# Operands of the recurrences turned tokens-first by VectorE and a DRAM round trip instead of by TensorE, with decays and late turnings put elsewhere

## The chip, the cores and the metric

The kernel runs on one core of a Trainium2 chip. The metric is the time of one execution on the device, in microseconds; lower is better. One profiled execution gives the trace that the profile is made of.

## The reference, cut to what matters

One step of a two-layer hybrid trunk with D = 2048: 256 prompt tokens from a zero state and 8 sequences of 8 sample tokens from given states, 320 tokens in all. Layer 0 projects the normalised input once and runs two recurrences on parts of it; layer 1 is a gated linear recurrence (RG-LRU). All is float32.

```python
proj = einsum('btd,de->bte', rmsnorm(x), w_in)          # Q, K, V of DeltaNet; gates; Q, K, V of GLA ...
q, k, v = silu(causal_conv(qkv))                        # 8 heads x 128
q = q * rsqrt(sum(q*q) + 1e-6) * 128**-0.5
k = k * rsqrt(sum(k*k) + 1e-6)
beta = sigmoid(b_raw);  g = -exp(a_log) * softplus(a_raw + dt_bias)
# gated delta rule, S (128 x 128) for each head:
S_t = exp(g_t) S_{t-1} (I - beta_t k_t k_t^T) + beta_t k_t v_t^T;   o_t = S_t^T q_t
# GLA, S (128 x 256) for each of 4 heads, gk = log_sigmoid(lr @ w_lr + b_lr) / 16:
S_t = diag(exp(gk_t)) S_{t-1} + k_t v_t^T;                          o_t = S_t^T q_t
x = x + concat(rmsnorm(o_a)*silu(z_a), rmsnorm(o_b)*silu(z_b)) @ w_out
x = x + (rg_lru(conv(x w_x)) * silu(x w_g)) @ w_lru_out
```

The delta rule is computed in chunks: with decays, k k^T and q k^T of a chunk give a triangular matrix, whose inverse is applied to the values. Final states and convolution histories are outputs too.

## The kernel before, in words

Activations lie with channels on the 128 partitions and tokens along the free dimension. The dense work is 30 groups of 512 output columns. A group has eight 512 KB weight chunks, loaded on SyncE's DMA queue (`wst`, three buffers, `load_chunk`, L214); each half of a chunk is split into a high and a low part, `wh` by ScalarE (L248) and `wl` by VectorE (L249), with six buffers each, and every product is three matmuls of 128x128 by 128x320 on L382 (xh wh, xl wh, xh wl). That is 5760 matmuls, called the main products here, and they run from beginning to end of the program. The groups come in the order Q0, K0, V0, V1, K1, Q1 (DeltaNet's, first and second half of the heads), QB, KB, VB, VB (GLA's), four gate groups, four of w_out, eight of the RG-LRU's input and four of its output.

Everything else is woven between them. The recurrences are Python generators in queues (`hi`, `lo`, `lo2`, `tails`). After every third main product `slot()` advances each queue by one step, and the table `WAITS` says for how many slots a named step waits. So the order on TensorE is written out by this table; a tile scheduler adds the semaphores, and each engine then runs its list in order. PSUM has four buffers for the groups (`acc`) and four that all the woven work shares in turn (the helpers `bank` and `bank4`): a matmul into such a buffer waits until the result four uses before has been read.

The woven work that the change touches:

- `delta_half(0)` and `delta_half(1)`: four heads each, in two chunks of 128 tokens (a "quad" is four heads of one chunk). `quad_a` turns K, Q and V tokens-first by TensorE transposes with an identity (`kt` L720, `qt` L729, `vt` L771), sums squares of K and Q on ScalarE, makes the decays between tokens (`ug` L746 on VectorE, `df` and `gr` L755 on TensorE, `dtm` and `eg` on ScalarE), then `kk` (L777) and `kq` (L789), times the decays into `bt` and `mt`. `nb`, minus beta over the norm of k, is turned (`nbt` L799) and stored. `invert32` loads the diagonal blocks from DRAM (`bd_scratch`), multiplies them by `nb` (L827) and inverts them on GpSimd; `quad_front` builds the whole inverse XT; `quad_b` and `quad_end` apply it (`y` L966) and make outputs and state.
- `delta_sample` does the same for the 8 sample sequences, with the states loaded into `st` on SyncE's queue (L1032), and the chain bt, inversion on VectorE, XT, `y` (L1074), `pq` (L1081), `ot` (L1105).
- `gla_decays` makes GLA's cumulated decays (`lrp` L1338 on TensorE, `gk`). `gla_head` turns V of GLA by TensorE (`gvt` L1443) and uses it in `gpo` (L1450) and `gsn` (L1454).

## Time and profile before

| | |
|---|---|
| runs (three) | 975.67, 975.74, 976.48 us; median 975.74 |
| profiled execution: time, span of its instructions | 975.99 us, 973.8 us |
| mean granted TensorE clock | 0.998 |
| TensorE busy | 963.4 us, 99% of the span |
| VectorE, ScalarE, GpSimd busy | 693.9, 532.8, 193.3 us |
| main products, mean duration as listed | 5568 of 128x320 on L382, 310 to 313 ns |

A matmul's listed duration is from its start to its result; several are in flight at once, so what one costs TensorE is the distance to the next start. An engine's idle time is put down to whatever released the instruction after it. The line numbers are those of the kernel before, unless a text says otherwise.

### The profile page before, as it was taken

How to read it: one execution, taken by the hardware profiler on the slowest of the kernel's cores; microseconds unless marked ns; L12 is line 12 of the kernel's file. 1: busy time of each engine (PE TensorE's matmuls, PEld its weight loads, DVE VectorE, ACT ScalarE, POOL GpSimd, SP SyncE). 2: the span in 40 equal slices, each digit the busy share in tenths (PEclk: the TensorE clock that was granted, in tenths of full speed). 3: DMA queues.
4: the chain of work that ended last, by engine and by line, in shares of the span. 5: the costliest groups of instructions: out<-in, count | busy, mean ns of one | idle time of the engine just before them, and what ended most of it. 6: DMA issues, size and time to landing. Idle time of an engine off the chain costs nothing.

```text
span 973.8 us, 18776 instructions
## 1 busy us (share of the span) xinstructions
PE 963.4 (99%) x6921; PEld 947.0 (97%) x6921; DVE 693.9 (71%) x1470; ACT 532.8 (55%) x1089; POOL 193.3 (20%) x336
## 2 busy tenths in 40 slices
PE   9999999999999999999999999999999999999996
PEld 9999999999999999999989999999999999999996
DVE  7598887666545556788668789667969668876763
ACT  7767865447333454876423345348685885333452
POOL 4010128403381011120105124100010000042200
PEclk9999999999999999999999999999999999999999
DMA  9854444533545366444587877654435435677742
GB/s 323 296 172 130 136 129 149 169 108 122 151 152 153 98 229 222 126 130 130 193 277 231 258 239 252 202 154 154 154 127 180 132 129 169 190 228 252 265 170 109
DMA packets 68123, 175.03 MB, mean 180 GB/s; under 512 B 17116, under 2 KB 26096, under 8 KB 67520
## 3 DMA queue, kind: packets, MB, share of 16 engines
q1 hardware_dynamic: 62904, 163.69, 52.8%
q0 software_dynamic: 2720, 8.66, 2.5%
q10 hardware_dynamic: 2408, 1.49, 0.5%
q8 instruction: 54, 0.88, 0.4%
q14 instruction: 37, 0.30, 0.1%
HBM read 159.14 MB, written 14.68 MB: 178 GB/s over the span
## 4 chain that ended last, share of the span: by engine, by line
PE 97%; DVE 1%; DMA 0%; issue 0%; ACT 0%; SPq 0%; POOL 0%; DVEq 0%; ACTq 0%; POOLq 0%
PE acc L382 83%; PE acc L268 3%; PE fbt L311 1%; PE gpo L1500 0%; DMA ob<-in_x_cols_dram 0%; PE lg L1689 0%; PE lg L1687 0%; PE lg L1688 0%; PE kq L789 0%; PE kk L777 0%; PE gsn L1263 0%; PE po L975 0%; PE pq L1063 0%; PE sn L1249 0%; PE y L966 0%
## 5 line engine op out<-in xcount | busy, mean ns | idle before, releaser
L382 PE MATMUL acc<-xh,wh 128*128 128x320 f32 x1856 | 580.1, 313 | 0.3 <-ACT wh L235 0.3
L382 PE MATMUL acc<-xl,wh 128*128 128x320 f32 x1856 | 574.3, 310 | 0.0
L382 PE MATMUL acc<-xh,wl 128*128 128x320 f32 x1856 | 573.4, 310 | 0.3 <-DVE wl L249 0.3
L248 ACT ACTIVATE wh<-wst 128x512 fp32r<-128x512 f32 x479 | 278.9, 624 | 299.1 <-PE acc L382 251.7
L249 DVE TENSOR_TENSOR wl<-wst,wh 128x512 fp32r<-128x512 f32 x479 | 331.6, 722 | 150.8 <-ACT wh L248 148.5
L382 PEld LDWEIGHTS acc<-xh,wh 128*128 128x128 f32 x1856 | 348.8, 188 | 3.4 <-issue 1.3
L382 PEld LDWEIGHTS acc<-xl,wh 128*128 128x128 f32 x1856 | 348.7, 188 | 1.1
L382 PEld LDWEIGHTS acc<-xh,wl 128*128 128x128 f32 x1856 | 348.2, 188 | 1.1 <-DVE wl L249 0.5
L590 DVE SCALAR_TENSOR_TENSOR yc<-slab,pa,yc 128x344 f32<-128x344 f32 x72 | 40.5, 575 | 3.0 <-ACT yc L102 2.7
L834 POOL TENSOR_TENSOR xi<-xi,tmp 128x60 f32<-128x60 f32 (+24 forms) x62 | 26.1, 421 | 4.9
L832 POOL TENSOR_TENSOR tmp<-ab,xi 128x60 f32<-128x60 f32 (+24 forms) x62 | 24.7, 398 | 4.8
L1716 POOL MEMSET aa<- 128x32 f32 x4 | 0.6, 162 | 117.7 <-ACT rr L1703 66.7
L1144 POOL TENSOR_TENSOR uvkh<-uvk,uvkh 32x256 fp32r<-32x256 f32 (+1 forms) x8 | 10.7, 1342 | 51.5 <-DVE uvkh L1140 50.6
L1149 POOL TENSOR_TENSOR uvm<-uvh,rm 96x512 fp32r<-96x512 f32 x16 | 19.5, 1241 | 2.8 <-PE sn L1249 2.5
L1253 DVE SCALAR_TENSOR_TENSOR ust<-ust,es,sn 128x128 f32<-128x128 f32 x64 | 18.2, 337 | 2.5 <-PE sn L1249 2.2
L889 POOL TENSOR_TENSOR so<-so,mhalf 128x4 f32<-128x4 f32 x4 | 4.4, 1104 | 74.0 <-DVE so L888 74.0
L268 PE MATMUL acc<-xl,wh 128*128 128x320 f32 (+1 forms) x64 | 18.7, 292 | 0.0
L268 PE MATMUL acc<-xh,wl 128*128 128x320 f32 (+1 forms) x64 | 18.7, 292 | 0.0
L594 ACT ACTIVATE qkv<-yc 128x256 f32<-128x256 f32 x24 | 10.0, 415 | 15.9 <-DVE yc L590 15.8
L268 PE MATMUL acc<-xh,wh 128*128 128x320 f32 (+1 forms) x64 | 18.6, 291 | 0.0
L1267 DVE SCALAR_TENSOR_TENSOR ugt<-ugt,ebs,gsn 128x256 f32<-128x256 f32 x32 | 14.1, 474 | 5.6 <-PE gsn L1263 5.5
L1647 DVE SCALAR_TENSOR_TENSOR yc<-slab,pb,yc 128x344 f32<-128x344 f32 x32 | 17.5, 569 | 0.6 <-ACT yc L1645 0.5
(465 smaller groups left out, 1053.1 us busy)
## 6 DMA issues: line engine op xcount, KB each, us to landing
wst<-in_w_dense_dram SPq DMA_DIRECT2D x237, 512.0 KB, 3.7
st<-in_state_delta_dram SPq DMA_DIRECT2D x8, 512.0 KB, 7.0
st<-in_state_gla_dram SPq DMA_DIRECT2D x4, 1024.0 KB, 6.9
ust<-in_state_delta_dram SPq DMA_DIRECT2D x8, 512.0 KB
out_s_delta_dram<-ust POOLq DMA_DIRECT2D x8, 512.0 KB, 4.7
ugt<-in_state_gla_dram SPq DMA_DIRECT2D x8, 512.0 KB, 5.5
out_s_gla_dram<-ugt POOLq DMA_DIRECT2D x8, 512.0 KB, 4.3
xtok<-in_x_rows_dram SPq DMA_DIRECT2D x6, 512.0 KB, 6.3
```

The costliest lines, as they stand in the source:

```text
L248: act.activation(h, wst[i][:, a, :], AF.Copy)
L249: env["last_split"] = dve.tensor_sub(l, wst[i][:, a, :], h.bitcast(F32))
L268: mm = pe.matmul(accs[f][:, cols], w[:, fs], x[:, cols], start=(k == 0 and j == 0), stop=(k == KT - 1 and j == 2), skip_group_check=True)
L382: mm = pe.matmul(o, (h, h, l)[j][:, fs], (xh, xl, xh)[j][k], start=(k == 0 and j == 0), stop=(k == KT - 1 and j == 2))
L590: dve.scalar_tensor_tensor(y[:, :n], xp[:, j:j + n], pa[:, ft, j:j + 1], y[:, :n], op0=OP.mult, op1=OP.add)
L832: behind(pool.tensor_mul(tv, ab[:, j, j + 1:, None].to_broadcast([P, m, w]), xi[:, j:j + 1, :w].to_broadcast([P, m, w])))
L834: behind(pool.tensor_add(xi[:, j + 1:, :w], xi[:, j + 1:, :w], tv))
L1144: pool.tensor_sub(o, t[rows, :, cols], o.bitcast(F32))
L1149: pool.tensor_mul(m, src.bitcast(F32)[:, None, :].to_broadcast([R, 4, P]), rm4[:R, :, None].to_broadcast([R, 4, P]))
L1253: dve.scalar_tensor_tensor(s_, s_, es[:, col:col + 1], ps[:, b, :], op0=OP.mult, op1=OP.add)
L1267: dve.scalar_tensor_tensor(s_, s_, ebs[:, h, 4 * hb + b + i:4 * hb + b + i + 1], ps[:, i * 256:(i + 1) * 256], op0=OP.mult, op1=OP.add)
L1647: dve.scalar_tensor_tensor(y[:, :n], xp[:, j:j + n], pb[:, ft, 2 + j:3 + j], y[:, :n], op0=OP.mult, op1=OP.add)
```

## The change

Eighty-one TensorE transposes are removed: `kt`, `qt`, `vt` (20 each), `nbt` (5) and `gvt` of V (16). In their place `turn` transposes 32x32 blocks on VectorE with a strided source (44 instructions), into a staging tile; SyncE's queue stores it to a DRAM scratch (`tp_scratch` for prompt tokens, `ts_scratch` for samples), and `load_turned` loads it back with its rows in tokens-first order, in runs of 512 bytes. The loaded tiles hold [token, block of 32, head, 32], so `y`, `gpo` and `gsn` read them in runs of 32 elements.

Beside this: the squares of K and Q are summed from the loaded tiles; the factor `nb` goes into `dtm` (four scalings on VectorE per quad), so that `nbt`, its store and load, and the multiplication by `bn` before the inversions go; `quad_front`'s scaling becomes a copy, half of it on ScalarE; the second chunk's `ug` is made by GpSimd; `gla_decays` starts 70 slots after its flag instead of 11; V of the first half and Q of the second half are turned and loaded after the quads (`rest`); the blocks for the inversion are stored and loaded in fewer, larger transfers; and the samples' states are loaded on ScalarE's queue.

```diff
...
-    "small_work.1": 0, "small_work.2": 2, "small_work.3": 10, "quad_a.1": 2, "quad_a.2": 8, "quad_a.3": 0,
+    "small_work.1": 0, "small_work.2": 2, "small_work.3": 10, "delta_sample.9": 3, "turn.4": 40, "turn.5": 0, "delta_sample.3": 3, "quad_a.1": 8, "quad_a.2": 2, "quad_a.3": 0,
...
+    "turn.1": 3, "turn.2": 6, "turn.3": 10, "quad_a.8": 10, "gla_decays.3": 5, "gla_decays.4": 1, "gla_decays.5": 3, "gla_decays.6": 3, "gla_decays.7": 6, "gla.1": 0,
-    "tables.2": 14, "small_work.4": 3, "small_work.5": 9, "gla_decays.8": 11, "quad_b.9": 1,
+    "tables.2": 14, "small_work.4": 3, "small_work.5": 9, "gla_decays.8": 70, "quad_b.9": 1,
...
-    nb_d = nc.dram_tensor("nb_scratch", (20, P), F32, kind="Internal").ap()
+    tp_d = nc.dram_tensor("tp_scratch", (8, 2, P, 4 * P), F32, kind="Internal").ap()
+    ts_d = nc.dram_tensor("ts_scratch", (3, 1, P, 4 * P), F32, kind="Internal").ap()
...
+    def turn(src, d, flag, to, gate, first):
+        yield from wait(first)
+        while gate not in env["done"]:
+            yield
+        n = src.shape[2] // P
+        to = to.rearrange("p f t -> p (f t)")[:, :4 * P * n].rearrange("p (c x) -> p c x", c=n)
+        for f in range(4):
+            behind(dve.transpose(to.rearrange("p c (b u j) -> p u c b j", u=4, j=32)[:, f],
+                                 src[:, f, :].rearrange("p (c i b) -> p c b i", c=n, b=4)))
+            yield from wait("turn.1")
+        yield from wait("turn.2")
+        behind(sp.dma_start(d.rearrange("c p x -> p c x"), to))
+        yield from wait("turn.3")
+        env["done"].add(flag)
+    def load_turned(out, d, c=0):
+        sp.dma_start(out.rearrange("p a u j -> p a (u j)"), d[c].rearrange("(a i) (b x) -> (i b) a x", a=4, b=4))
+    def turn_conv(part, half, to, gate):
+        first = "turn.4" if (part, half) in ((2, 0), (0, 1)) else "turn.5"
+        src = env["QKV"[part], half]
+        turns.append(turn(src, tp_d[2 * part + half], ("t", part, half), to, gate, first))
+    def turn_sample(part):
+        src = env["SMP" + "QKV"[part]].rearrange("p u q e x -> p u (q e x)")
+        turns.append(turn(src, ts_d[part], ("t", part, "s"), ob[3], "gd", "turn.5"))
...
+            def turned():
+                if part or half:
+                    turn_conv(part, half, ob[1], "x0")
+                if part == 1 and half == 0:
+                    turn_conv(0, 0, ob[0], "x0")
+                if half:
+                    turn_sample(part)
+            hi.append(later(turned))
...
+        turned = lambda part: (tp_d[2 * part + half], c) if q.n == 32 else (ts_d[part], 0)
         ss = t("ss", [P, 8])
-        ps = bank4("kt")
-        for u in range(U):
-            pe.transpose(ps[:, u, :], q.k(u), ident)
-        q.ktm = t("ktm")
-        act.activation(q.ktm, ps, AF.Copy)
-        for u in range(U):
-            j = t("junk", [P, P], 1)
...
-        ps = bank4("qt")
-        for u in range(U):
-            pe.transpose(ps[:, u, :], q.q(u), ident)
...
+        rows = lambda nm, tag=None: t(nm, [P, 4, 4, 32], tag=tag)
+        kin = rows("kin", "mt")
+        if q.n < 32:
+            q.bt = t("bt")
+        load_turned(kin, *turned(1))
+        late = {0: 2, 1: 0}.get(half)
+        if late != 0:
+            qin = q.bt.rearrange("p u (a j) -> p u a j", j=32)
+            load_turned(qin, *turned(0))
+        if late != 2:
+            q.rv = rows("rv")
+            load_turned(q.rv, *turned(2))
         if q.n == 32:
...
-            ug = ws.tile([P, 2, 4, P], F32R, name="ug", tag="ab", bufs=1)
+            ug = ws.tile([P, 2, 4, P], F32R, name="ug", tag=("ab", "XT")[c], bufs=1)
...
-            dve.tensor_mul(ug[i], q.um[:, None, :].to_broadcast([P, 4, P]),
+            (pool if c else dve).tensor_mul(ug[i], q.um[:, None, :].to_broadcast([P, 4, P]),
...
+        q.ktm = t("ktm")
+        act.activation(q.ktm.rearrange("p u (a j) -> p a u j", j=32), kin, AF.Copy)
+        for u in range(U):
+            j = t("junk", [P, P], 1)
+            act.activation(j, q.ktm[:, u, :], AF.Square, accum_out=ss[:, u:u + 1])
...
+        def v_scale():
+            dve.tensor_mul(q.rv, q.rv, q.bk[:, None, :, None].to_broadcast([P, 4, 4, 32]))
+        dve.tensor_scalar(sk, sk, EPS, None, op0=OP.add)
+        dve.reciprocal(q.nb, sk)
+        dve.scalar_tensor_tensor(q.nb, q.nb, -1.0, beta[:, q.gc:q.gc + 4], op0=OP.mult, op1=OP.mult)
+        for u in range(U):
+            dve.scalar_tensor_tensor(dt[:, u, :], dt[:, u, :], q.nb[:, u:u + 1], q.um, op0=OP.mult, op1=OP.mult)
+        pool.tensor_tensor(q.bk, sk, mhalf[:, :4], OP.pow)
+        pool.tensor_mul(q.bk, q.bk, sk)
+        pool.tensor_scalar(q.bk, q.bk, -1.0, None, op0=OP.mult)
...
-        ps = bank4("vt")
-        for u in range(U):
-            pe.transpose(ps[:, u, :], q.v(u), ident)
-        q.rv = t("rv")
-        scaled4(q.rv, ps, q.bk, NA0)
-        yield from wait("quad_a.4")
...
-        ps = bank("nbt")
-        pe.transpose(ps[:4, :P], q.nb, ident)
-        nbt = t("nbt", [4, P], 1)
-        act.activation(nbt, ps[:4, :P], AF.Copy)
-        pool.dma_start(nb_d[q.id:q.id + 4, :], nbt)
...
+        def rest():
+            while ("t", late, half) not in env["done"]:
+                yield
+            x = rows("rv") if late else rows("qin", "pt")
+            load_turned(x, *turned(late))
+            yield from wait("quad_a.8")
+            if late:
+                q.rv = x
+                v_scale()
+            else:
+                q_sums(x)
+            env["done"].add(("rows", q.id))
+        if late is not None:
+            lo2.append(rest())
...
-        pool.tensor_mul(ab, ab, bn[:, None, :].to_broadcast([P, n, n]))
...
-        def scale(ps, rows, w):
-            for c, q in enumerate(qs):
-                dve.tensor_mul(pt[c][rows, :, :w], ps[rows, 4 * c:4 * c + 4, :w],
-                               q.nb[rows, :, None].to_broadcast([rows.stop - rows.start, 4, w]))
+        def keep(ps, rows, w):
+            dve.tensor_copy(pt[0][rows, :, :w], ps[rows, 0:4, :w])
+            act.activation(pt[1][rows, :, :w], ps[rows, 4:8, :w], AF.Copy)
...
-            pe.matmul(ps[:, u, :], q.xt[:, u, :], q.rv[:, u, :], start=True, stop=True)
+            pe.matmul(ps[:, u, :], q.xt[:, u, :], q.rv[:, :, u, :], start=True, stop=True)
...
+            yield from wait("delta_half.2")
+            for b, bs in enumerate(blocks):
+                sp.dma_start(bd_d[us, b].rearrange("u j i -> j u i"), bt[bs, :, bs])
...
-                    sp.dma_start(st[:, e], state_delta[2 * u + e])
+                    act.dma_start(st[:, e], state_delta[2 * u + e])
+            yield from quad_a(q, ws, 1)
+            inverse = invert(ws, 4, 8)
+            next(inverse)
+            yield from wait("delta_sample.9")
             load(0)
             load(1)
-            yield from quad_a(q, ws, 1)
-            yield from invert(ws, 4, 8)
+            yield from inverse
             load_inv(q, ws)
...
+                if pr == 0:
+                    yield from wait("delta_sample.3")
+                    load(2)
+                    load(3)
...
-            pt = bank4("gvt")
-            for hf in range(2):
-                vt = 2 * h + hf
-                pe.transpose(pt[:, hf, :], env["VB", vt // 4][:, vt % 4, cs], ident)
-            pe.transpose(pt[:, 2, :], kd[128][:, cs], ident)
-            vk = t("gvk", [P, 3, P])
-            act.activation(vk, pt[:, :3], AF.Copy)
+            pt = bank("gvt")
+            pe.transpose(pt[:, :P], kd[128][:, cs], ident)
+            vk = t("gvk", [P, P])
+            act.activation(vk, pt[:, :P], AF.Copy)
             yield from wait("gla.3")
             po = bank("gpo")
-            vtm = vk[:, 0:2, :].rearrange("p a b -> p (a b)")
-            pe.matmul(po[:, :256], at, vtm, start=True, stop=not c)
+            split = lambda x: x[:, :256].rearrange("p (f a j) -> p f a j", f=2, j=32)
+            vtm = vt[c][:, :, 2 * (h % 2):2 * (h % 2) + 2, :].rearrange("p a f j -> p f a j")
+            pe.matmul(split(po), at, vtm, start=True, stop=not c)
             if c:
...
-                yield from weave(gla_head(h, ws), gla_head(h + 1, ws))
+                while ("t", "VB", h // 2) not in env["done"]:
+                    yield
+                vt = [ws.tile([P, 4, 4, 32], F32, name="gvv", tag="gvv", bufs=4) for _ in range(2)]
+                for c in range(2):
+                    load_turned(vt[c], tp_d[6 + h // 2], c)
+                yield from weave(gla_head(h, ws, vt), gla_head(h + 1, ws, vt))
...
```

Three places of the order. First TensorE at the first two quads (half 0), with the main products between the rows left out. Before:

```order
L755 MATMUL df<-ug,sl_r 128x512 x2
L771 MATMUL vt<-ident,qkv 128x128 x4
L777 MATMUL kk<-qkv 128x128 x4
L789 MATMUL kq<-qkv 128x128 x4
L799 MATMUL nbt<-ident,nb 4x128
L382 MATMUL acc<-xh_118,wh 128x320
L382 MATMUL acc<-xl_134,wh 128x320
L382 MATMUL acc<-xh_118,wl 128x320
L755 MATMUL df<-ug,sl_r 128x512 x2
L755 MATMUL gr<-ug,ones_r 128x512 x2
```

With the change:

```order
L794 MATMUL df<-ug,sl_r 128x512 x2
L794 MATMUL gr<-ug,ones_r 128x512 x2
L384 MATMUL acc<-xh_117,wh 128x320
L384 MATMUL acc<-xl_133,wh 128x320
L384 MATMUL acc<-xh_117,wl 128x320
L1409 MATMUL lrp<-lr_231 128x320
...
L831 MATMUL kk<-qkv 128x128 x4
L838 MATMUL kq<-qkv 128x128 x4
L831 MATMUL kk<-qkv 128x128 x4
L838 MATMUL kq<-qkv 128x128 x4
```

The first df stands three main products ahead of this piece, and six more main products stand where rows are left out. kk and kq of both quads are now one after another, after both df; a row of GLA's decays (lrp) has come between, and the transposes are gone.

Second, TensorE at the samples' first two head pairs: the end of pq, its output's transpose ot, and the second pair's pq. Before, with 36 main products between the first two rows:

```order
L1081 MATMUL pq<-y_4877,mt 128x256 x2
...
L1105 MATMUL ot<-ident,on 128x128 x2
L382 MATMUL acc<-xh_111,wh 128x320
L382 MATMUL acc<-xl_127,wh 128x320
L382 MATMUL acc<-xh_111,wl 128x320
L1063 MATMUL pq<-st,qm 32x128 x32
```

With the change, 22 main products:

```order
L1153 MATMUL pq<-y_4776,mt 128x256 x2
...
L1177 MATMUL ot<-ident,on 128x128
L1130 MATMUL pq<-st,qm 32x128
L1177 MATMUL ot<-ident,on 128x128
L1130 MATMUL pq<-st,qm 32x128 x31
```

ot follows its pq sooner, and the second pair's pq follows ot at once.

Third, SyncE's queue around the first half's quads. Before:

```order
L214 DMA wst<-in_w_dense_dram 128x1024 x7
L784 DMA bd_scratch<-bt 32x4x32 x8
L214 DMA wst<-in_w_dense_dram 128x1024
L821 DMA ab<-bd_scratch 32x1024 x2
L522 DMA out_dconv_dram<-stc 128x108
L821 DMA ab<-bd_scratch 32x1024
```

With the change:

```order
L565 DMA tp_scratch<-ob_138 128x2x512
L216 DMA wst<-in_w_dense_dram 128x1024
L571 DMA bt<-tp_scratch 128x4x128 x2
L216 DMA wst<-in_w_dense_dram 128x1024 x4
L1055 DMA bd_scratch<-bt 32x8x32 x4
L883 DMA ab<-bd_scratch 32x1024 x4
L216 DMA wst<-in_w_dense_dram 128x1024 x3
```

One weight load stands between the store of the turned Q and the two loads that wait for it; the block stores are four instead of eight, and their loads follow them at once.

124 lines of the change are left out of this document (60 added, 64 removed), and 11 rows, old and new, of the table WAITS.

## The prediction

> **What bounds the kernel now.** I read the page's first part, then the chain that ended last, then TensorE's waits.
>
> ```profile
> span 973.8 us, 18776 instructions
> PE 963.4 (99%) x6921; PEld 947.0 (97%) x6921; DVE 693.9 (71%) x1470; ACT 532.8 (55%) x1089; POOL 193.3 (20%) x336
> PE 97%; DVE 1%; DMA 0%; issue 0%; ACT 0%; SPq 0%; POOL 0%; DVEq 0%; ACTq 0%; POOLq 0%
> ```
>
> TensorE is busy for 99% of the span and is 97% of the chain. Its waits by line say the same:
>
> ```profile
> PE frs L354 <- DVE rr L352: 1.4, 1, 1.4
> PE got L1310 <- DVE gon L1306: 1.2, 2, 0.6
> PE warm L1840 <- DVE mhalf L1826: 1.1, 1, 1.1
> ```
>
> Two of the three lie at the program's start and end; between them it has only got's 1.2 us to gain from other engines. So there are two ways to change the time: give TensorE less to issue, or make it wait. What an instruction of TensorE is worth is the distance between starts, not its duration. The timeline of TensorE where the first four transposes of K stand among the main products (start, duration, engine, line):
>
> ```profile
> 109.54 0.31 PE L382 MATMUL acc<-xh,wl 128*128 128x320 f32 x1
> ...
> 109.98 0.31 PE L382 MATMUL acc<-xh,wl 128*128 128x320 f32 x1
> 110.12 0.60 PE L720 MATMUL kt<-ident,qkv 128*128 128x128 f32 x4
> 110.48 0.39 PE L382 MATMUL acc<-xh,wh 128*128 128x320 f32 x1
> 110.71 0.31 PE L382 MATMUL acc<-xl,wh 128*128 128x320 f32 x1
> ```
>
> Main products start every 0.147 us (three steps in 109.98 - 109.54). From 109.98 to 110.71 lie two main products and four transposes: 0.73 - 2 x 0.147 = 0.44 us, so **0.11 us a transpose**.
>
> **What leaves TensorE.** The groups of TensorE by line and shape (columns: busy us, mean ns):
>
> ```profile
> L720 PE MATMUL kt<-ident,qkv 128*128 128x128 f32 x16 | 2.2, 273 | 0.0
> L729 PE MATMUL qt<-ident,qkv 128*128 128x128 f32 x16 | 2.4, 272 | 0.0
> L771 PE MATMUL vt<-ident,qkv 128*128 128x128 f32 x16 | 2.4, 272 | 0.0
> ...
> L720 PE MATMUL kt<-ident,smpK 128*128 128x128 f32 x4 | 0.6, 272 | 0.0
> ...
> L799 PE MATMUL nbt<-ident,nb 128*4 128x128 f32 x5 | 1.4, 273 | 0.0
> L1443 PE MATMUL gvt<-ident,gp 128*128 128x128 f32 x16 | 3.1, 273 | 0.0
> ```
>
> The samples have a quad of each of K, Q and V, so 3 x 16 + 3 x 4 + 5 + 16 = 81 transposes go; the other matmuls stay, in number and size. 81 x 0.11 = **8.9 us less**. For this to be whole, nothing that replaces them may make TensorE wait.
>
> The Trainium skill, "TensorE: Matmul & The Clock Gate", Part 4, gives a TensorE transpose about 275 ns in a kernel and 390 ns alone (bf16). The trace agrees with the first as a duration, but not as a price: the next instruction starts 0.11 us later. With 275 ns for each, by that page, the estimate of the gain would be 22 us; the pitch decides.
>
> **What replaces them** is 44 VectorE transposes (32 of 128x256, 12 of 128x128), 11 stores and the loads from DRAM. Nearest rows for the first, and VectorE's busiest stage (columns there: us, then busy us of PE, PEld, DVE, ACT, POOL):
>
> ```profile
> L914 DVE STREAM_TRANSPOSE xz<-xc 32x256 f32<-32x256 f32 x4 | 1.7, 431 | 0.1
> L1604 DVE TENSOR_REDUCE sq<-sq 128x320 f32<-128x1280 f32 x3 | 7.4, 2473 | 0.3
> 96.00:125.00 29.00, 29.00 (x204) 28.49 (x203) 25.15 (x54) 24.91 (x71) 4.36 (x7) 1.00 0.48 146
> ```
>
> A transpose of 256 elements has a row, 0.43 us, but with contiguous reads; here the source is read with a step of four. The one strided read shown, the reduction, takes 2473/1280 = 1.93 ns an element. So 0.43 to 256 x 1.93 = 0.49 us by that row, and up to 0.8 us if the step nearly doubles it. 44 of them are 16 to 35 us, against 973.8 - 693.9 = 280 us in which VectorE is free. I take the lower half, and nothing on the path: they are spread over four groups of some 30 us, and V of half 0 and Q of half 1 come after the quads, outside the tight stage shown (3.9 us free of 29). Scaling dtm by four 128x128 operations a quad instead of one of 128x512, less the multiplies that leave, is some 3 us more, hidden likewise.
>
> The second chunk's ug moves to GpSimd, where a two-input operation of 96x512 takes over a microsecond:
>
> ```profile
> L1149 POOL TENSOR_TENSOR uvm<-uvh,rm 96x512 fp32r<-96x512 f32 x16 | 19.5, 1241 | 2.8 <-PE sn L1249 2.5
> L249 DVE TENSOR_TENSOR wl<-wst,wh x20: 691/754/2906, 141.5 to 175.6; 128x512 fp32r<-128x512 f32 x20
> ```
>
> The second row is wl (minimum, median, longest, ns) while GpSimd inverts: VectorE can be held for 2.9 - 0.7 = 2.2 us. Four operations so held are 0 to 9 us of VectorE; wl is made some 36 main products (5 us) before its use, which covers each hold once. I take 0.
>
> The Trainium skill, "SBUF — State Buffer", section "Who interferes with whom", says that a VectorE instruction with two SBUF inputs contends with a GpSimd instruction that reads SBUF, for its whole length. The longest wl agrees. By the rule the four operations could hold one wl each, which still fits its lead.
>
> **Where the freed time makes waits.** With fewer instructions between them, four results now come later than TensorE asks.
>
> First quads. Now df, gr, lrp and then kk, kq, kk, kq of both quads stand within 12 main products, and each takes a PSUM buffer from one of the results ahead. Today they stand apart:
>
> ```profile
> 120.67 0.62 PE L755 MATMUL df<-ug,sl_r 128*128 128x512 f32 x2
> 120.87 1.28 ACT L763 ACT_TABLE_LOAD   x1
> ...
> 122.16 0.60 ACT L763 ACTIVATE dtm<-df 128x512 f32<-128x512 f32 x1
> ...
> 125.25 0.59 ACT L761 ACTIVATE eg<-gr 128x512 f32<-128x512 f32 x1
> ...
> L1340 DVE TENSOR_SCALAR gk<-lrp,pc 128x320 f32<-128x320 f32 x4 | 2.2, 547 | 1.4 <-ACT ob L1339 1.4
> ```
>
> From the first df at t, ScalarE is done with dtm at 122.76 - 120.67 = t + 2.1, with eg and the second dtm at t + 3.3, then wh and lrp, 0.6 and 0.5 more; gk takes 0.55 after it: t + 5.0. TensorE reaches the second kq after the second df and gr (two matmuls each of 512 columns, 0.147 x 512/320 = 0.235: 0.94 in all), 12 main products (1.8), lrp (0.15) and three sets of four of 128 columns (0.44 each, as the transposes): t + 4.2, counted from the first df's end at 0.5 after t: t + 4.7. Wait 0.3; with VectorE's six scalings of 0.34 queued between, up to 1.5, and 0 if lrp is read earlier. I take **0.7**. The second half has the same order without lrp: **0.2** (0 to 0.5).
>
> The samples' inverse. The chain bt, inversion, XT, y, seen today:
>
> ```profile
> 353.53 0.38 SPq L786 DMA_DIRECT2D bt_scratch<-bt  x1
> 367.90 0.38 SPq L878 DMA_DIRECT2D XT<-xt_scratch  x1
> XT<-xd_scratch SPq DMA_DIRECT2D x16, 16.0 KB, 1.6
> wst<-in_w_dense_dram SPq DMA_DIRECT2D x237, 512.0 KB, 3.7
> 382.16 1.95 PE L1063 MATMUL pq<-st,qm 128*32 128x128 f32 x64
> ```
>
> Store to load takes 14.4 us; 256 KB land in between 1.6 and 3.7: 16.0 to 18.1. The change leaves 93 main products and the 64 small matmuls of pq between store and y: 13.7 + 1.95 = 15.6. Wait 0.4 to 2.5, less a small multiply by bn that goes from the chain. I take **0.8** (0 to 2), low because st loads no longer stand in SP's queue there.
>
> The samples' output. From pq to ot, today:
>
> ```profile
> 375.26 1.02 PE L1081 MATMUL pq<-y,mt 128*128 128x256 f32 x4
> 378.18 1.04 POOL L1091 TENSOR_TENSOR so<-so,mhalf 128x4 f32<-128x4 f32 x1 [8.27 <-DVE so L1089]
> 379.53 0.62 ACT L102 ACTIVATE on<-pq,so 128x128 f32<-128x128 f32 x2 [0.96 <-POOL so L1094]
> 380.24 0.61 DVE L1100 SCALAR_TENSOR_TENSOR on<-pq,so,on 128x128 f32<-128x128 f32 x2 [0.94 <-ACT on L102]
> 381.40 0.38 PE L1105 MATMUL ot<-ident,on 128*128 128x128 f32 x2
> ```
>
> pq ends at 376.28, on at 380.85: 4.6 us, under 36 main products (5.3). Now 22 stand between, 3.2 us: **1.4** (1.0 to 1.8). What is queued behind ot on TensorE is the second pair's pq and the main products.
>
> **Sum**: 975.99 - 8.9 + 0.7 + 0.2 + 0.8 + 1.4 = 970.2 for a profiled execution; the median of the runs is 0.25 lower than it (975.74): **969.9**. With no wait 966.8, with all at their upper ends (5.8) 972.6.
>
> **Rivals.** (A) The places that I cannot price add up: the scheduler's tight spots cost another 2 to 4 us (gla's first products behind the loads of V, quad_front behind ScalarE's half of keep): 971.9 to 973.9. For it: new operands come by a queue. Against: ScalarE and VectorE wait long for TensorE.
>
> (B) Slower. SP's queue is blocked by round trips. A load from DRAM waits at the head of SP's queue until its store has landed, and weight loads stand behind it.
>
> ```profile
> SPq L214 <- DVE wl L249: 563.9, 194, 8.6
> out_s_delta_dram<-ust POOLq DMA_DIRECT2D x8, 512.0 KB, 4.7
> ```
>
> A 512 KB store takes 4.7 us; a weight load waits for its buffer, not for the queue, for 563.9/194 = 2.9 us. If all seven places block for the whole 4.7, weights come 7 x 1.8 = 12.6 us late: 969.9 + 12.6 = 982.5. It decides from (5.8 + 2)/7 = 1.1 us beyond the lead at each. Against: two or more weight loads stand between a store and its load, and today's ScalarE hardly waits for weights.
>
> (C) The strided moving operand. y and GLA's products now read runs of 32 elements. Nothing today reads so; if they took twice as long, 40 y x 0.11 + 32 products of 256 columns x 0.22 = 11.3 us: 981.2. Not at all, or half of that, is as open by the rows; runs of 128 bytes make me think it nothing.
>
> (D) The transposes cost their whole duration, 81 x 0.272 = 22 us: 975.99 - 22 + 3.1 - 0.25 = 956.8. The pitch speaks against.
>
> (E) The transposes were hidden, so nothing goes: 975.7 plus 3.1. Against: 97% of the chain.
>
> **How the numbers follow.** Forecast 0.62 (966.8 to 971.9), A 0.18, B 0.10, C 0.05, D 0.01, E 0.04. About 0.2%, 2 us, is what a measurement of this kernel can tell from no change. A divides into 0.17 faster and 0.01 same; B into 0.06 slower, 0.03 same and 0.01 faster (fewer places blocked); C into 0.01 slower, 0.02 same (half of it, 975.5) and 0.02 faster; E into 0.02 slower and 0.02 same. Faster (below 973.8): 0.62 + 0.17 + 0.01 + 0.01 + 0.02 = 0.83. Same: 0.01 + 0.03 + 0.02 + 0.02 = 0.08. Slower: 0.06 + 0.01 + 0.02 = 0.09. The range 966.5 to 974.5 leaves out no more than 2 in 10; its lower end is the sum without waits, its upper reaches past A.
>
> **What would show it.** Right: kt, qt, vt, nbt and VB's gvt gone from TensorE's groups; its busy time some 9 us less; new waits of TensorE at ot (line 1177) about 1.4, at y (1146) and at kq (838) under 1.5 each; wl and wh hardly there. y's and gpo's pitch unchanged speaks against C. Wrong: a wait of acc for wl or wh of several microseconds with SP idle at the loads of turned rows (B), or VectorE's transposes at 0.8 us and the wl behind them late.

## The result: 0.7% slower, and the profile after

The changed kernel takes 982.93 us (median of 4 runs, 981.82 to 984.68) against 976.11 us of the kernel before (4 runs, 975.67 to 977.52): **1.0069 times as long, 95% interval 1.005 to 1.0088**. The forecast was 969.9 us, faster. The profiled execution took 984.68 us, 8.7 more than that of before.

Its page, first and fourth part:

```profile
span 982.8 us, 18647 instructions
PE 959.8 (98%) x6840; PEld 941.7 (96%) x6840; DVE 712.3 (72%) x1523; ACT 527.3 (54%) x1078; POOL 194.0 (20%) x333
PE 47%; DMA 1%; DVE 1%; issue 0%; POOL 0%; ACT 0%; DVEq 0%; SPq 0%; ACTq 0%; POOLq 0%
```

The 81 transposes are gone (6921 matmuls before, 6840 now), yet TensorE's busy time fell by only 3.6 us and the span grew by 9.0. (The shares of the second line add to 49%: this chain could be followed back to 499 us only, so its 47% does not compare with the 97% of before.) TensorE's waits by line (columns: us in total, times, longest):

```profile
PE acc L384 <- DVE zs L1602: 3.2, 1, 3.2
PE acc L384 <- DVE smpvb L1356: 2.2, 1, 2.2
PE acc L384 <- DVE wl L251: 1.4, 2, 0.9
...
PE acc L384 <- DVE slab L484: 1.3, 1, 1.3
...
PE acc L384 <- ACT wh L237: 1.2, 1, 1.2
PE ot L1177 <- DVE on L1172: 1.1, 1, 1.1
...
PE kk L831 <- ACT dtm L802: 0.9, 1, 0.9
PE kq L838 <- ACT dtm L802: 0.8, 1, 0.8
...
PE y L1146 <- DMA XT<-xt_scratch: 0.3, 1, 0.3
```

Left out are rows that the kernel before has too, and one of 0.3 us. The last four are the waits that the prediction had priced. The large ones are others: main products (`acc`) that wait for VectorE to read an earlier group out of PSUM (`zs`, `smpvb`, `slab` are such evacuations; lines 1602, 1356, 484). VectorE's own waits tell why it was late:

```profile
DVE tmp L918 <- DMA ab<-bt_scratch: 5.8, 1, 5.8
DVE xz L963 <- DMA xc<-xd_scratch: 4.6, 1, 4.6
```

Neither load is new. In the kernel before VectorE has no listed wait for `xc`, and for `ab` this one:

```profile
DVE ab L857 <- DMA ab<-bt_scratch: 0.6, 1, 0.6
```

The timeline of the stop for `xc` in the changed kernel, all engines:

```profile
290.93 0.38 SPq L1062 DMA_DIRECT2D xc<-xd_scratch  x1
...
293.61 0.88 DVE L963 STREAM_TRANSPOSE xz<-xc 32x256 f32<-32x256 f32 x2 [4.59 <-DMA xc<-xd_scratch]
...
296.52 0.21 DVE L1356 TENSOR_TENSOR smpvb<-acc,rb 128x64 f32<-128x64 f32 x1
...
296.88 0.38 PE L384 MATMUL acc<-xh,wh 128*128 128x320 f32 x1 [2.22 <-DVE smpvb L1356]
```

VectorE runs its list in order. Its next instruction was the transpose of `xc`, a load that SyncE issued at 290.93; it stood still for 4.59 us until that had landed, with the evacuations of the finished group's four accumulators behind it; and TensorE, whose next group starts in the first of these, stood still for 2.22. The other place is the samples' inverse, where the loads of `ab` (4 KB each, SyncE's queue) were issued together with the second pair of states (512 KB each, now on ScalarE's queue):

```profile
363.93 2.76 SPq L911 DMA_DIRECT2D ab<-bt_scratch  x4
364.11 4.60 ACTq L1095 DMA_DIRECT2D st<-in_state_delta_dram  x4
...
372.16 0.16 DVE L918 TENSOR_TENSOR tmp<-ab,xi 64x7 f32<-64x7 f32 x1 [5.77 <-DMA ab<-bt_scratch]
```

And each of the two long stops cost more than itself. TensorE's timeline right behind the first, and the windows of the changed kernel and of the kernel before (columns: window, length, busy us of PE, PEld, DVE, ACT, POOL, then the granted clock, DMA share, GB/s):

```profile
297.24 0.31 PE L384 MATMUL acc<-xh,wl 128*128 128x320 f32 x1
...
297.90 0.47 PE L384 MATMUL acc<-xh,wh 128*128 128x320 f32 x1
298.16 0.47 PE L384 MATMUL acc<-xl,wh 128*128 128x320 f32 x1
298.43 0.47 PE L384 MATMUL acc<-xh,wl 128*128 128x320 f32 x1
```

```profile
295.00:300.00 5.00, 3.12 (x14) 3.15 (x15) 5.00 (x14) 0.26 (x1) 0.00 (x0) 0.77 0.66 197
300.00:305.00 5.00, 5.00 (x32) 5.00 (x32) 2.73 (x5) 1.15 (x2) 0.00 (x0) 0.89 0.29 108
...
375.00:380.00 5.00, 4.25 (x18) 4.19 (x19) 5.00 (x15) 2.35 (x3) 0.00 (x0) 0.66 0.41 110
```

```profile
295.00:300.00 5.00, 5.00 (x36) 5.00 (x35) 2.94 (x6) 1.94 (x4) 0.31 (x1) 1.00 0.57 196
```

Main products start every 0.147 us up to 297.7 and every 0.265 from 297.9 to 301.1. The granted clock is 0.77 and 0.89 in the ten microseconds of the first stop and 0.66 behind the second; before it was 1.00. That is (0.23 + 0.11 + 0.34) x 5 = 3.4 us more.

So the account of the profiled execution: 81 transposes less at 0.106 (measured below), -8.6; new waits 12.1 (the rows above add to 12.4; `wh`, at the program's start, had 0.3 before); the clock 3.4. That makes +6.9 of the 8.7. An estimate of most of the rest: a listed wait begins at the end of the matmul ahead of it, 0.31 us after its start, where the next would have started after 0.147, so each stop costs 0.16 us beyond its row, and the changed kernel has nine more of them: 1.5 us.

### The profile page after: what moved, and what is told of

The parts are those of the page before. It is cut to its first block, busy times and chain, and to the rows that moved or that the text cites. A ratio compares the mean times of both kernels' runs of the same rounds, so it can differ in the third digit from the quotient of the medians.

```text
span 982.8 us, 18647 instructions
## 1 busy us (share of the span) xinstructions
PE 959.8 (98%) x6840; PEld 941.7 (96%) x6840; DVE 712.3 (72%) x1523; ACT 527.3 (54%) x1078; POOL 194.0 (20%) x333
## 5 line engine op out<-in xcount | busy, mean ns | idle before, releaser
L892 POOL TENSOR_TENSOR tmp<-ab,xi 128x60 f32<-128x60 f32 (+24 forms) x62 | 27.3, 440 | 32.1 <-DMA ab<-bd_scratch 27.5
```

What stands on the lines that cost most here:

```text
L892: behind(pool.tensor_mul(tv, ab[:, j, j + 1:, None].to_broadcast([P, m, w]), xi[:, j:j + 1, :w].to_broadcast([P, m, w])))
```

## Experiments: one wait at a time

The question was whether the places named above cause the loss. Each of the first kernels takes away what makes one of them wait.

**The transposes of `xc` in `quad_front` placed behind the main product that is being issued**, so that VectorE meets them later:

```diff
-            dve.transpose(dst[cut(b)], xc[cut(b)])
+            behind(dve.transpose(dst[cut(b)], xc[cut(b)]))
...
-        dve.transpose(x[cut(1), :, n:], xc[cut(1)])
+        behind(dve.transpose(x[cut(1), :, n:], xc[cut(1)]))
```

> The changed kernel, with only quad_front's three VectorE transposes of xc placed later in VectorE's order (beside lp, which needs them, some 85 main products later), so that they no longer stand there before xc has landed. Theory T (VectorE stands still at a load from DRAM, with the evacuations of acc queued behind it): VectorE's wait xz <- xc (4.6 us) goes, TensorE's wait for smpvb (2.2 us) goes, and the slow clock from 297 to 303 us (granted 0.77 and 0.89) with it: 3 to 4.5 us less than the changed kernel, 978.5 to 980. Rival R1 (VectorE is overloaded by its transposes): the evacuations are late all the same, TensorE waits there 1 us or more, time within 1.5 us of 983. Rival R2 (weights late): unchanged.

Measured: 983.59 us against 976.77, ratio 1.0071 (1.0058 to 1.0084). TensorE's waits:

```profile
PE acc L384 <- DVE zs L1602: 3.6, 1, 3.6
PE acc L384 <- DVE wl L251: 1.5, 3, 0.8
...
PE y L1146 <- DMA XT<-xt_scratch: 1.1, 1, 1.1
```

The wait for `smpvb` is gone, and so is the low clock behind it: from the start of the group ahead of the stop to the start of the group behind it TensorE gains 4.0 us on the changed kernel. But it had come there 1.8 us later, `zs` and `y` took 1.0 more behind it, and the span is 1.4 shorter in all. The mechanism of this stop is shown; its removal is not worth its size, and the 3 to 4.5 us that were expected do not come.

**V's scaling in `rest` placed likewise** (it made VectorE wait for V's turned rows ahead of `slab`):

```diff
-                v_scale()
+                behind(v_scale())
```

> The changed kernel, with only the first half's scaling of rv (late V) placed 17 main products later in VectorE's order. T: VectorE's wait rv <- tp_scratch (2.2 us in two) falls to under 0.5, TensorE's wait for slab (1.3 us at 161 us) goes: 1 to 1.5 us less, 981.5 to 982. R1: VectorE's load is the same there, so TensorE still waits about 1 us for slab; no change in time.

Measured: 985.9 against 976.77, ratio 1.0096 (1.0082 to 1.0111). `slab`'s wait is gone, and `lxt` (the first half's inverse, line 979) waits 1.6 us in its place.

**The second pair of states loaded later** (ten slots instead of three, and behind a main product), so that the small loads of `ab` meet no 2 MB of states:

```diff
-    "delta_sample.3": 3,
+    "delta_sample.3": 10,
...
-                    act.dma_start(st[:, e], state_delta[2 * u + e])
+                    i = act.dma_start(st[:, e], state_delta[2 * u + e])
+                    if u > 1:
+                        behind(i)
```

> The changed kernel, with only the second pair's four state loads (512 KB each, ScalarE's queue) issued some 30 main products (4.5 us) later, after the four small loads of ab instead of beside them. T with contention: ab lands 3 us or more sooner, VectorE's wait for it falls from 5.8 to under 2.5 us, TensorE's wait for zs (3.2 us) and the slow clock at 376 to 380 us go: 4 to 5 us less, 978 to 979; less the waits that pq's second pair may then have for its states (0 to 2 us). If ab's landing does not depend on the state loads (rival: its own small packets or the queue): VectorE still waits 5 us or more, time 982 to 985.

Measured: 991.79 against 976.77, ratio 1.0143 (1.0126 to 1.0161), the slowest of all but one:

```profile
PE y L1148 <- DMA XT<-xt_scratch: 4.8, 1, 4.8
PE acc L384 <- DVE smpvb L1358: 2.9, 1, 2.9
PE gvt L1562 <- POOL gvs L1561: 2.1, 1, 2.1
```

VectorE's wait for `ab` fell from 5.8 to 1.2 us and `zs` from 3.2 to 0.3, as the cause predicts. But XT now came behind the states, and `y` waited 4.8; GLA's sample part came later in its turn and waited for a buffer (`gvs`, 2.1).

**All three edits together.**

> The three edits together. T: the three waits go and no slow clock is left before 940 us; 983 - 4 - 1.3 - 4.5 = 973 (971 to 976), about 3 us under the kernel before. R1 or R2: 980 or more.

Measured: 986.52, ratio 1.0104 (1.009 to 1.0118). At the end of the eleventh group TensorE is 7.0 us ahead of the changed kernel, so the three stops are worth that; three and a half groups later it is 1.8 behind it, with `y` at 3.9 and `gvt` at 2.6.

**The changed kernel again, on another chip**, as a point of comparison for the next three.

> The changed kernel itself, for a comparison on one chip with the runs beside it: 981.5 to 984.5. If it comes out at 985 or more here, the chip, and not the edits, explains why the first four experiments came out above it.

Measured: 986.82 against 976.57, ratio 1.0098 (1.0084 to 1.0112). Its waits are those of the first time. Of the 2.7 us that its span is longer, 2.2 lie in the first half group; more on that below. The changed kernel's own median was 982.93 us the first time, 986.82 here and, below, 987.65, so a few microseconds between kernels measured apart from each other tell nothing; their waits do.

**State loads as before** (SyncE's queue, the old places):

```diff
-                    act.dma_start(st[:, e], state_delta[2 * u + e])
+                    sp.dma_start(st[:, e], state_delta[2 * u + e])
...
-                if pr == 0:
-                    yield from wait("delta_sample.3")
-                    load(2)
-                    load(3)
```

> The changed kernel, with the samples' state loads as they were before the change: on SyncE's queue, the first pair ahead of quad_a, the second pair at the end of the first pair's step. Theory T2 (the samples' chain through DRAM is late because the state loads now land beside its small loads): VectorE's wait for ab under 2.5 us (5.8 in the changed kernel), TensorE's waits for zs and y together under 1 us, no slow clock at 375 to 380 us; 4 to 5.5 us less than the changed kernel beside it. Rival (the chain is late because TensorE reaches its end sooner, wherever the states are loaded): the wait moves to y or to pq of the second pair and stays above 3 us; time within 1.5 us of the changed kernel.

Measured: 988.73, ratio 1.0117 (1.0104 to 1.013). Up to the middle of the twelfth group 2.9 us are gained, then 5.3 lost. The waits for `zs` and of `y` are gone but for 0.2; `acc` waits for VectorE's inversion 1.8, `ot` 2.7 in two, `got` 2.5 in four. VectorE's wait for `ab` is 3.3 us, where under 2.5 was expected: part of it is there without the states beside those loads.

**GLA's decays started as before.**

```diff
-    "gla_decays.8": 70,
+    "gla_decays.8": 11,
```

> The changed kernel, with only gla_decays back at its old start (11 slots instead of 70), so that its VectorE scans lie before the first quads and not in the stage with the V turnings. If VectorE's full stage at 132 to 148 us is what delays wl there: TensorE's two waits for wl (1.4 us together at 145 to 148 us) go, and the wait of kk at 120 us does not grow (0.9): 1 to 2 us less than the changed kernel. If the transposes alone or GpSimd's inversion delay wl: the waits stay above 1 us, time the same or, with decays and first quads together again, up to 2 us more.

Measured: 985.23, ratio 1.0091 (1.0077 to 1.0106). `wl` and `slab` no longer wait, `kq` waits 2.3 instead, with the clock low behind it. Of the 3.2 us that its profile is ahead of the one beside it, 1.9 lie at the start; no gain over the changed kernel can be told.

**The old places of the states, the placed `xc`, the old decays, and the first quads' steps moved, together.** The edits of three experiments above, and:

```diff
-    "quad_a.1": 8, "quad_a.2": 2,
+    "quad_a.1": 5, "quad_a.2": 5,
```

> The changed kernel with the state loads and gla_decays as before the change, the xc transposes placed beside lp, and df and gr three slots sooner (kk stays). T and T2 together: waits for zs, smpvb, wl, kk and kq all gone or under 0.5 us, no slow clock before 940 us: the changed kernel less 10 to 13 us, 970 to 973, under the kernel before. If the waits only move to the next result of each chain: 978 or more.

Measured: 986.73, ratio 1.0094 (1.0078 to 1.011):

```profile
PE lp L969 <- DVE xz L963: 4.0, 3, 3.2
PE ot L1170 <- DVE on L1165: 2.7, 2, 1.4
PE got L1377 <- DVE gon L1373: 2.5, 4, 1.0
PE acc L384 <- DVE xi L920: 1.8, 1, 1.8
PE y L1139 <- DMA XT<-xt_scratch: 1.7, 1, 1.7
```

The waits for `zs` (but for 0.2) and `smpvb` and those of `kk` and `kq` are gone (`slab` has 1.4 in two, `wh` 1.3, `wl` 0.5), and the same time stands at others. Where VectorE no longer stops for `xc`, TensorE itself stops for what is made of it (`lp`).

So in seven kernels the waits that were aimed at went or shrank, others came, and none was faster than the kernel before. That left two explanations: the new loads make waits wherever they are put, or the work at the side takes a fixed time, and TensorE, with less of its own work, always comes too soon to some result of it. They differ in what the transposes alone are worth.

## Experiments: the transposes without the scheme, and the scheme with the transposes

**76 transposes taken out of the kernel before, nothing in their place.** K, Q, V and GLA's V are read as they lie.

```diff
-        ps = bank4("kt")
-        for u in range(U):
-            pe.transpose(ps[:, u, :], q.k(u), ident)
+        ps = q.all("K")
```

and the same for `qt`, `vt` and two of three of `gvt`.

> The kernel before with 76 of the 81 transposes taken out and nothing in their place: K, Q and V of DeltaNet and V of GLA are read as they lie, channels first, by the same ScalarE and VectorE instructions (so the results are not the reference's; sizes and counts of all else stay; the five transposes of nb stay). It measures the first term of the sum by itself. Theory L (the loads of the new scheme make the waits): the removal is worth its pitch, 76 x 0.11 = 8.4 us, and no new wait of TensorE over 1 us comes: 967 to 969. Rival F (chains of fixed length: with less of its own work TensorE comes sooner to results that are no earlier, so the gain turns into waits whatever replaces the transposes): 973 to 976, with waits of TensorE for lp, y or wl of some 5 us in sum.

Measured: **975.93 against 976.03 us, ratio 0.9994 (0.9984 to 1.0005)**. The gain of 8 us does not come even where nothing replaces the transposes:

```profile
PE df L753 <- ACT dtm L761: 1.9, 1, 1.9
PE y L1070 <- DMA XT<-xt_scratch: 1.8, 1, 1.8
...
PE ot L1101 <- DVE on L1096: 1.2, 1, 1.2
```

Group by group the transposes do leave their price (2.55 us for the 24 of the first half), and these three waits and smaller ones take back all but 1.8 us of it in the profiled execution. The first of them is one of PSUM's buffers: with `kt`, `qt` and `vt` gone only `kk`, `kq` and `nbt` stand between the two `df` of the second half, so the second `df` takes, of the four buffers, the one that the first had, before `dtm` has read it. Transposes taken out are also results taken out of that ring.

**76 transposes put back into the changed kernel, unread.**

```diff
+            if nm == "df":
+                for u in range(U):
+                    pe.transpose(ps[:, P * u:P * u + P], q.k(u), ident)
```

and likewise ahead of `kk`, `kq` and `gvt`.

> The changed kernel with 76 transposes put back on TensorE that nobody reads: four of K, Q and V each ahead of df, kk and kq in the same PSUM buffers, and 16 of V of GLA; they are overwritten. All else as in the changed kernel, so this is the new scheme's cost without its gain. Theory L: the waits smpvb, zs and slab stay within 1 us of those of the changed kernel beside it, only kk, kq and wl behind them fall by up to 2 us in sum: 8.4 - 2 = 6 to 8.5 us above the changed kernel. Rival F: the waits fall by nearly all that is put back: 0 to 3 us above it.

**The changed kernel beside it.**

> The changed kernel itself on the same chip as the three others, as their point of comparison: 982 to 988, 0.6 to 1.1% above the kernel before.

Measured: 992.04 us with them, 987.65 without (ratios to the kernel before 1.0153, 1.0136 to 1.017, and 1.0108, 1.0092 to 1.0124): 4.4 us apart in the medians and 1.0 in the profiled spans, for 8 us of transposes.

```profile
PE y L1153 <- DMA XT<-xt_scratch: 2.6, 1, 2.6
PE acc L384 <- DVE slab L484: 2.3, 1, 2.3
```

The waits for `smpvb` and `zs`, 2.6 and 4.0 in the kernel beside it, are gone, and the clock falls only behind `slab`. Theory L had them stay within 1 us: it falls. For `smpvb` VectorE's list is the same in both, so there it is TensorE's pace alone: the inversion on GpSimd takes its time, and the transposes ahead of it (48 by then, 5 us) cover it. Rival F had said 0 to 3 us: the medians lie between the two theories, the profiled spans in F's range (this profiled execution is the shortest of its four, that beside it the longest of its four).

The other reading of this run is against the kernel before: 16.0 us slower in the medians, 13.8 in the profiled spans, with all but five of the transposes in TensorE's list. Some 11 us of new waits stand in it (the two rows above, `wl` 1.6, `kk` 1.3, `ot` 1.1 and smaller ones). So the new scheme makes TensorE wait by itself, also where TensorE comes no sooner than before.

**V of GLA alone, turned by VectorE and DRAM, in the kernel before.**

```diff
+                turns.append(turn(st["t"], tp_d[idx], ("t", "VB", idx), ob[3], ("a", 0), "turn.5"))
...
-                pe.transpose(pt[:, hf, :], env["VB", vt // 4][:, vt % 4, cs], ident)
...
+                for c in range(2):
+                    load_turned(vt[c], tp_d[h // 2], c)
```

> The kernel before with one part of the change alone: V of GLA is turned by VectorE (8 transposes of 128x256) and a round trip through DRAM, and 16 transposes leave TensorE; DeltaNet and all other places as before. Its loads have some 500 main products of lead, and no VectorE instruction reads them. Theory L: 16 x 0.11 = 1.8 us gained, waits of TensorE as before: 974.2 to 975.5 against 976.5 of the kernel before. Rival F: 976 to 977, the gain lost at got or gvt.

Measured: 981.47 against 976.03, ratio 1.0047 (1.0033 to 1.0062): slower, though DeltaNet is untouched. Its profiled execution took 978.2, the second shortest of ten, so it shows only part of the loss: `y` waits 1.1 and `ot` 1.2, as above.

In this kernel and in that with 76 transposes taken out, the lists had changed around the samples' inverse, which `WAITS` alone does not fix: a small change elsewhere had moved the whole step. The last copy of the inverse stood at main product 2106 instead of 2089, XT's load at 2130 instead of 2109 (on SyncE's queue, behind two of the second pair's state loads of 512 KB), and TensorE's own `y` at 2147 instead of 2133. So the next three runs asked whether that change of order is the cause.

**40 transposes (K and Q) taken out of the kernel before; here the arrangement stays.** The edits are those of the kernel without 76, for `kt` and `qt` alone:

```diff
-            pe.transpose(ps[:, u, :], q.k(u), ident)
...
-            pe.transpose(ps[:, u, :], q.q(u), ident)
```

> The kernel before with the 40 transposes of K and Q of DeltaNet taken out and nothing in their place (K and Q are read as they lie, so the results are not the reference's); V's and all others stay. Unlike in the run where 76 were taken out, the list of instructions keeps the order around the samples' inverse: its last copy stands at main product 2089 and y at 2133, as in the kernel before (there: 2106 and 2147). Theory O (the gain comes back where the order of the list flips): y and ot have no wait, 40 x 0.105 = 4.2 us gained less at most 1.9 at df: 970.5 to 972.5 profiled, the median 972 to 974. Rival F (chains of fixed length bind as soon as TensorE comes sooner): waits of y and ot of 3 us together all the same, 975 to 977.

Measured: **973.0 against 976.58 us, ratio 0.9962 (0.9951 to 0.9974)**: 3.6 us faster. `y` and `ot` do not wait. TensorE's new waits:

```profile
PE acc L382 <- ACT wh L235: 0.9, 1, 0.9
PE gpo L1498 <- DMA st<-in_state_gla_dram: 0.4, 1, 0.4
PE nbt L797 <- ACT dtm L761: 0.3, 1, 0.3
```

Over the stretches in which they stood, 16, 16 and 8 transposes leave 1.75, 1.75 and 0.86 us: **0.109 us each**, as the prediction read it from the pitch.

**V of GLA turned only behind the samples' second `y`**, so that all lists are those of before up to there.

```diff
-                turns.append(turn(st["t"], tp_d[idx], ("t", "VB", idx), ob[3], ("a", 0), "turn.5"))
+                turns.append(turn(st["t"], tp_d[idx], ("t", "VB", idx), ob[3], "y2", "turn.5"))
```

with the loads moved to just ahead of GLA's first products.

> V of GLA alone turned by VectorE and DRAM, as in the earlier run of that part, but its turning starts only behind the samples' second y, and its loads stand just ahead of their use. So the list of every engine is that of the kernel before up to main product 2208, and y and ot stand where they stood. Theory O: y and ot have no wait; 16 x 0.105 = 1.7 us gained, less up to 1 us where VectorE is tight ahead of GLA's first products: 974 to 976 profiled. Rival F: 976 to 979, with y and ot waiting as in the earlier run (1.1 and 1.2).

Measured: 979.31 against 976.58, ratio 1.0022 (1.0014 to 1.0031): less slow than the earlier placing, still not faster. (The profiled execution, 976.83, is the fastest of its twelve, so here too the trace shows little of the loss.) Theory O said that `y` would not wait; it waited 1.2 us:

```profile
353.33 0.39 SPq L810 DMA_DIRECT2D bt_scratch<-bt  x1
...
366.24 1.75 SPq L893 DMA_DIRECT2D xt_scratch<-ab  x4
...
371.22 0.38 SPq L902 DMA_DIRECT2D XT<-xt_scratch  x1
```

From the store of `bt` to the load of XT: 17.9 us here, with the order of before, where it was 14.4; 15.1 in the kernel without K's and Q's transposes, 16.3 in that without 76, 17.3 in the changed kernel. So the chain is of no fixed length either: two round trips through DRAM in it vary by 3 us and more from kernel to kernel. Why they were slow in this execution (the last store lay 3.2 us ahead of the load, against 1.1 before) stays open.

**16 transposes of GLA's V taken out, nothing in their place.** The kernel that ran first under this heading was not the one described: it was that with 76 taken out, and with `y` and `ot` asked for later:

```diff
-    "delta_sample.4": 8, "delta_sample.6": 8,
+    "delta_sample.4": 12, "delta_sample.6": 12,
```

> The kernel before with GLA's 16 transposes of V taken out and nothing in their place (V is copied as it lies, so the results are not the reference's). The order of all else is kept. Theory O: 1.7 us gained and no new wait: 974.3 profiled, median within 0.5 of it. Rival F: 975.5 to 976.5, the gain lost at got.

Measured, for that other kernel: 977.41 against 976.58, ratio 1.0007 (0.9998 to 1.0016). `ot`'s wait is gone, `y`'s is 2.1, and the stretch of GLA behind them takes 3.8 us more than in the kernel with 76 taken out, with new waits for `uvm` (0.9) and `ob` (0.5); why is not shown. The one described ran next; its edit takes out the two lines of `gvt` that turn V.

> The kernel before with GLA's 16 transposes of V taken out and nothing in their place (V is copied as it lies, so the results are not the reference's). The order of all else is kept. Theory O: 1.7 us gained and no new wait: 974 to 975 for the median. Rival F: 975.5 to 976.5, the gain lost at got.

Measured: 975.51 against 976.33, ratio 0.9991 (0.9982 to 1.0): by the median in F's range, at its edge. Past the first half group its profile gains 1.53 us, 0.096 a transpose, with no new wait, which is Theory O's account. So GLA's part is worth 1.5 us, and by the medians its round trip costs more than that in either place.

**A version without a round trip: Q's sums by products with a column of ones.**

```diff
-        ps = bank4("qt")
+        ps = bank("qt")
         for u in range(U):
-            pe.transpose(ps[:, u, :], q.q(u), ident)
+            pe.matmul(ps[:, u:u + 1], sq[:, u, :], ones[:, :1], start=True, stop=True)
```

where `sq` is Q squared by GpSimd.

> The kernel before, where the 20 transposes of Q serve only the sums of squares of its rows: GpSimd squares Q as it lies (one 128x512 multiply a quad), and TensorE sums it by 20 matmuls with the squares as weights and one column of ones as the moving operand, in the places of the transposes; one small copy of ScalarE takes the place of four squarings. All results are the reference's; the order of the list stays. A matmul of one column against 128 may cost as much (if the loading of 128 weights sets the pitch of 0.11 us) or next to nothing. Theory O: 0 to 20 x 0.105 = 2.1 us gained, no new wait: 974 to 976.5. Rival F: slower, 977 to 979, with a wait at qt for GpSimd's squares of over 1 us.

Measured: 978.86 against 976.33, ratio 1.0025 (1.0016 to 1.0034), in the time of Rival F, but without its wait:

```profile
L733 PE MATMUL qt<-ones,sq 128*128 128x1 f32 x40 | 4.7, 239 | 0.0
```

There is no new wait. Each float32 product counts as two matmuls (40 for 20; the transposes were 20), and eight products in the first half cost 0.92 us more than the eight transposes: 0.22 against 0.11 each. So here a matmul with one moving column costs as much as one with 128, and there are two of them.

No version that computes the reference was faster than the kernel before.

## Why the prediction was wrong

- **The gain was sized right.** "0.11 us a transpose", 8.9 us in all: 0.109 and 0.096 measured, 8.6 us. The duration (rival D) was no price.
- **The priced waits were right in kind**: `kk` and `kq` 0.9 + 0.8 together against 0.7 + 0.2, `y` 0.3 against 0.8, `ot` 1.1 against 1.4. That their sum is the forecast 3.1 is luck. The second half's 0.8 lies outside its 0 to 0.5, and the chain to `y` took 20.9 us from the store of `bt`, not 16.0 to 18.1; `y` waited so little because TensorE stood 3.2 us for `zs` and lost 1.7 to the clock in the same stretch.
- **VectorE's transposes were sized right**:

```profile
L561 DVE STREAM_TRANSPOSE ob<-qkv 128x256 f32<-128x256 f32 x24 | 14.7, 624 | 0.0
L561 DVE STREAM_TRANSPOSE ob<-gp 128x256 f32<-128x256 f32 x8 | 5.0, 629 | 0.0
```

 0.62 us for 256 elements, between the bounds 0.43 and 0.8; some 24 us in all.
- **The step that failed is "I take the lower half, and nothing on the path"**, with the sentence ahead of it, "for this to be whole, nothing that replaces them may make TensorE wait". I weighed VectorE's new work against the 280 us that it is free in. What it lost is time in which it is neither busy nor free: it stands at the head of its list for a load (5.8 and 4.6 us, and 2.2 for V), and evacuations of PSUM stand behind it. In the sum's terms: new waits that no term named took 9.0 us (12.1 less the 3.1) and the clock 3.4. The two long stops are at loads that the kernel before has too, so a list of what is new would not have shown them. The row to ask was not the busy time but which instruction of VectorE waits for a load, how late that load can land, and whether a group of TensorE ends meanwhile: between the last product into a group's first accumulator and the next group's first product, which takes its buffer, the kernel has 18 main products, some 2.5 us, and that much of a stop there is hidden at most (4.59 us cost 2.22).
- **Second, the moved loads were not followed.** The states went to ScalarE's queue, and I priced that as relief for SyncE's. Together with them the last of the four 4 KB loads took 5.9 us to land, which is the longest stop of all. The Trainium skill, "DMA: Bandwidth & Descriptors", section "Latency and other measured facts", states that memory access is slower at high load; by the trace, VectorE's wait for the same loads was 0.6 us before and 5.8 beside 2 MB of states, which agrees; with the states issued later it was 1.2, but on their old queue and in their old places 3.3, so the load beside them is not all of it.
- **Third, the sum assumed that time taken from TensorE's list is gained unless a named result is late.** With 76 transposes taken out and nothing added the kernel gains 0.1 us. What TensorE gains in one place it meets, in part, as a wait at the next result. 40 transposes gained 3.6 of 4.3 us, 76 gained nothing: the slack of these chains is some microseconds at most. (With 76 the lists had changed as well, so how much of it is slack and how much order stays open.) "The chain is 97% TensorE" says that no one else is late at the present pace, not by how much they could be hurried. That bound I did not work out; it was to be had from the 19.5 us from the store of `bt` to `y` before, of which 14.4 stood before XT's load and 3 to 6 were its landing (3.0 and 5.9 where `y` waited for it).
- **The rivals.** A, small places adding up, had the right nature and a price of 2 to 4 us where 9 was due besides the clock. B, weights late behind round trips, was the rival on the right side, and its 982.5 is luck: `wl` and `wh` wait 1.4 and 1.2 us, not 12.6. C is refuted: from a `y` to the next start it is 0.11 us and from a `gpo` 0.215, in both kernels. E was named for another mechanism (hidden behind another engine at once) and dismissed with the 97%; for the bare removal of 76 its size, no gain, is what came.

## What to carry to other kernels

When a kernel is bound by one engine and everything else is tuned to be just in time, work out for each result that the bound engine asks for how much earlier it could be had, before counting on time taken from that engine; the smallest of these bounds what a removal can gain there. When an operand comes through DRAM, look at the in-order engine that reads it first: price the wait at the head of its list and what is queued behind it, not its busy time. And compare the arrangement of all engines' lists before and after, not that of the bound engine alone.

## What the runs showed of the hardware that was not expected

**A stop of TensorE can cost the clock.** At both long stops of the changed kernel the granted clock falls to 0.50 for about 3.4 us (behind the first, from 297.7 to 301.1), and main products start every 0.265 us instead of 0.147; two stops (5.4 us) cost 3.4 us more that way. Over all runs, up to the last 20 us of the program, no stop of under 1.8 us came with a fall and every one of over 2.7 us did; between them both happened: the clock fell behind stops of 1.8 (`xi`, with the states loaded as before), 2.0 and 2.1 us, and stayed at 1.00 behind others of 1.8, 1.9, 2.1 and 2.3 and behind one of 2.6 (`y` in the kernel with the transposes put back). The Trainium skill, "TensorE: Matmul & The Clock Gate", Part 1, says that the clock is halved after an idle window of about 3.4 us, and that the window runs freely. The trace agrees with the halving (granted clock 0.50), not with the length as a bound, since 1.8 us was enough once; that a longer stop once cost nothing fits a window whose phase is not the kernel's, which no run here shows.

**The program's start has two lengths.** The kernel of the last but one experiment came 1.9 us later out of the first half group than the kernel before, with the same instructions there. Its timeline (TensorE and ScalarE):

```profile
5.72 0.42 ACT L235 ACTIVATE wh<-wst 128x256 fp32r<-128x256 f32 x1 [1.80 <-DMA wst<-in_w_head_dram]
...
6.20 0.90 PE L382 MATMUL acc<-xh,wh 128*128 128x320 f32 x2 [1.15 <-ACT wh L235]
...
9.29 0.47 PE L382 MATMUL acc<-xl,wh 128*128 128x320 f32 x1
9.56 0.47 PE L382 MATMUL acc<-xh,wh 128*128 128x320 f32 x1
```

The second weight chunk landed 1 us later (5.72 against 4.75 before), TensorE stood 1.15 us instead of 0.27, and its matmuls then came every 0.27 us up to 9.8. So 1 us of a late load became 1.9; 0.27 is the pitch of the low clock above, though the profile lists no low clock there. A stop alone does not do it: the changed kernel stood 1.17 us at the same place, went on at 0.147 and left the first half group no later than the kernel before. Of all kernels four leave it 1.8 to 2.0 us later, the others at most 0.6. It accounts for the 1.9 to 2.2 us by which profiles that are alike up to there differ; for the spread of the timed runs, which carry no trace, that is likely and not shown.
